# Unread products that shift where each expert's main path begins in TensorE's program

## The chip, the cores and the metric

One of the eight cores of a Trainium2 chip runs the kernel. The time is the device time of one execution, from start to end, in microseconds (us).

## What is computed

One layer of a streaming encoder over 256 tokens of width 1024: a mixer (short convolution, two kinds of attention) and then a mixture of 32 experts, of which each token takes four. The part that matters here is the experts:

```
logits = (xt @ router_w + router_b)
top_vals, top_idx = lax.top_k(logits, 4)
top_w = jax.nn.softmax(top_vals, axis=-1)
combine = jnp.einsum('tk,tke->et', top_w, one_hot(top_idx, 32))
# for each expert e, summed over e:
u = xt @ w1 + b1
a = glu * jax.nn.sigmoid(1.702 * glu) * (lin + 1)     # of the clamped halves of u
acc = acc + gate_e[:, None] * (a @ w2 + b2)
```

Everything is float32. An expert's weights are 12 MB (w1 8 MB, w2 4 MB), and all 32 are read from HBM in every execution.

## The kernel before

The mixer runs first (until about 180 us of the profile), and the weights of the first experts are loaded behind it. Then the 32 experts run one after the other. The router's result is compacted: of each expert the first 64 tokens (CAP) are done by a **main path** that always runs; what is over 64 is done by up to four further blocks (MORE: 32, 64, 64 and 32 slots from slot 64, 96, 160 and 224), each inside the one before it, under a branch on the expert's token count. This whole nest, `if_more`, stands in the program ahead of the expert's main path, so an expert with 64 tokens or fewer jumps over it. Every engine reads the count and branches for itself. TensorE alone gets a hint on the branch (`hint`, a BRANCH_PREFETCH_HINT that says that the jump over the nest is likely to be taken); it stands at the start of the main path of the expert before.

In TensorE's program an expert's section is: the nest (four blocks, never all run), the hint, the bias product (`u<-b,pick`), the first half of w1 (`first`, tiles `u<-we,xg`), for even experts the scatter of the pair before (`y<-o,sc`), the second half of w1, the read of the next expert's count, for odd experts the gather for the next pair (`xg<-oh,xn`), the products with w2 (`o<-we,aT`) with transposes (`aT`) between them, and the next expert's branch. A product of float32 operands stands in the trace as two weight loads and two products, and a transpose or a bias product as one of each.

Weights come in 1 MB transfers from SP's queue (`prefetch`, line 858), 12 for each expert, into a ring of 20 buffers (RING). A transfer is issued when TensorE has read the buffer's last content, and SP's program keeps them in order: while SP waits for one buffer, nothing behind it is issued. The order of instructions is recorded by a scheduler from the Python program; `queue` and `issue_after` pin single steps. The lines are those of the profile: 83 is every product, 86 every transpose, 1021 the branch with its semaphores, 858 the weight transfers.

Of the kernel before, what the change touches and what calls it, by code (L numbers as in the profile page):

```python
# [18 lines left out]
P = 128  # L19
# [13 lines left out]
KINDS = {"l": 7, "h": 8, "x": 2, "c": 3}  # L33
RING = "lhhllccchlhhhxhhlllx"
CAP = 64
MORE = ((64, 32), (96, 64), (160, 64), (224, 32))


# [11 lines left out]
def trunk(ctx: ExitStack, tc: tile.TileContext, x_d, p1_d, p2_d, be_d, ada_d, win_d, wout_d, w1_d, w2_d, out_d):  # L50
# [26 lines left out]
    def pb(name):  # L77
        return psB.tile([P, 512], F32, tag="B", name=name)
# [6 lines left out]
    def turn(out, in_):  # L85
        last[:] = [nc.tensor.transpose(out, in_, ident).ins]  # L86
# [37 lines left out]
    ident = const.tile([P, P], F32, name="ident")  # L124
# [36 lines left out]
    SEL6 = SELE[:, 0:6]  # L161
    slots = const.tile([P, CAP + 32], F32, name="slots")
    iote = const.tile([P, NE], F32, name="iote")
# [565 lines left out]
    def onehot(oh, base, m, es, pos):  # L729

        at = slots[:, base:base + m].rearrange("p (o c) -> p o c", o=1).to_broadcast([P, len(es), m])
        nc.vector.tensor_tensor(oh, at, bcast(pos[:, es[0]:es[0] + len(es)], m), op=ALU.is_equal)

    def gather(ps, oh, t, w, ks=range(KD)):

        for k in ks:
            mm(ps[k * w // 512][:, k * w % 512:k * w % 512 + w], xn2[:, t, k * P:(k + 1) * P], oh.rearrange("p e c -> p (e c)"),
               t == 0 and k * w % 512 == 0, t == NT - 1)

    def modulated2(xg, ps, w):  # L740
        for k in (0, 4, 1, 5, 2, 6, 3, 7):
            o = xg[:, k].rearrange("p e c -> p (e c)")
            x = ps[k * w // 512][:, k * w % 512:k * w % 512 + w]
            if k > 3:
                nc.vector.tensor_scalar(o, x, s2[:, k:k + 1], t2[:, k:k + 1],  # L745
                                        op0=ALU.mult, op1=ALU.add)
            else:
                nc.scalar.activation(o, x, AF.Identity, scale=s2[:, k:k + 1], bias=t2[:, k:k + 1])  # L748
# [10 lines left out]
    class Prepare:  # L759


        def __init__(self, e):
            self.e = e
            self.oh = sm.tile([P, NT, 2, CAP], F32, tag="part", name=f"oh{e}")
            if e:
# [5 lines left out]
        def half(self, t, ks=range(KD)):  # L771
            if 0 in ks:
                onehot(self.oh[:, t], 0, CAP, [self.e, self.e + 1], pos[:, t])
            gather(self.ps, self.oh[:, t], t, 2 * CAP, ks)

        def rest(self):
            e = self.e
            xg = sm.tile([P, KD, 2, CAP], F32, tag="xg", bufs=1, name=f"xg{e}")
            modulated2(xg, self.ps, 2 * CAP)
            og = sm.tile([P, NT, 2, CAP], F32, tag="part", name=f"og{e}")  # L780
# [238 lines left out]

    def if_more(n_e, e, a, aT, blocks=MORE):  # L1020
        with tc.If(n_e > blocks[0][0], label=f"few{e}") if blocks is MORE else tc.If(n_e > blocks[0][0]):  # L1021
            more(e, a, aT, *blocks[0])
            if blocks[1:]:
                if_more(n_e, e, a, aT, blocks[1:])

    @contextmanager
    def behind_branch():
# [19 lines left out]
    def tokens(e):  # L1047

        traced = nc.cur_bb.bb.instructions
        n = len(traced)  # L1050
        value = nc.values_load(cnt[0:1, e:e + 1], min_val=0, max_val=S)
        return value, next(i for i in traced[n:] if i.engine == mybir.EngineType.PE)

    late = None
    n_next, _ = tokens(0)
    for e in range(NE):
        if e:
            prefetch(4)
        xg, sc, _ = ready[e]
        aT = [t1k(f"aT{e}_{G}").rearrange("p (j s) -> p j s", j=2) for G in range(2)]  # L1060
        n_e = n_next
        if_more(n_e, e, t1k(f"am{e}", "partp"), t1k(f"aTm{e}"))
        with behind_branch():
            if e + 1 < NE:
# [27 lines left out]
    o, sc, _ = late  # L1092
# [72 lines left out]
```

## Time and profile before

| what | us |
|---|---|
| median of three runs | 1147.12 |
| lowest and highest run | 1146.0, 1147.28 |
| profiled execution, its own time | 1146.89 |
| its span, first to last instruction | 1144.9 |
| TensorE busy | 1069.5 (93%) |
| mean HBM traffic over the span | 391 GB/s |

The profiled execution's own time is 2.0 us over its span, and 0.23 us under the median. "PEq" in an idle note is TensorE's sequencer: the engine waited for an instruction of line 1021 that the sequencer itself works on. Numbers of experts run from 0 to 31.

### The profile page before, as it was taken

What the parts mean: (1) busy time and instruction counts of PE and PEld (TensorE: products, weight loads), DVE (VectorE), ACT (ScalarE), POOL (GpSimd) and SP (SyncE); (2) the same over time, 40 slices, a digit from 0 to 9 for tenths busy, and PEclk for the clock granted to TensorE, in tenths of its full rate; (3) what the DMA queues carried; (4) which work ended last, traced back from release to release, by engine and by line L of the source; (5) the groups of instructions that cost most, each with busy time, mean ns of one, the idle gap of its engine ahead of it and who ended that gap; (6) DMA issues with size and microseconds to landing.
All of it is one profiled execution on the core that took longest, in us unless ns stands there. A gap on an engine that the chain in (4) does not pass through costs nothing. (4 is left out here: it accounts for less than half of the span.)

```text
span 1144.9 us, 14101 instructions
## 1 busy us (share of the span) xinstructions
PE 1069.5 (93%) x5432; PEld 467.1 (41%) x5432; DVE 389.2 (34%) x879; ACT 178.6 (16%) x412; POOL 14.5 (1%) x52
## 2 busy tenths in 40 slices
PE   2999999999989999999999989999999999898987
PEld 2887844343333333433333433434343434242322
DVE  7799933222232223222222222232232322231222
ACT  3458622010101010101010100101010101010100
POOL 1000000000000000000000000000000000000000
PEclk7899999999999999999999989999999999999999
DMA  9888899999987999999999999999999999999992
GB/s 383 360 297 311 331 409 370 416 418 417 418 353 309 417 418 417 418 418 417 417 418 416 419 399 404 419 418 418 417 417 419 417 418 417 411 416 410 416 413 110
DMA packets 62913, 449.54 MB, mean 393 GB/s; under 512 B 6960, under 2 KB 7472, under 8 KB 8624
## 3 DMA queue, kind: packets, MB, share of 16 engines
q1 hardware_dynamic: 62336, 447.11, 95.6%
q8 instruction: 79, 1.29, 0.5%
q10 hardware_dynamic: 432, 0.59, 0.1%
q14 instruction: 66, 0.54, 0.1%
HBM read 446.63 MB, written 1.05 MB: 391 GB/s over the span
## 5 line engine op out<-in xcount | busy, mean ns | idle before, releaser
L83 PE MATMUL u<-we,xg 128*64 128x512 f32 (+1 forms) x2304 | 494.2, 577 | 12.7 <-DMA we<-in_w 11.3
L83 PEld LDWEIGHTS u<-we,xg 128*64 128x64 f32 (+1 forms) x2304 | 154.0, 134 | 299.9 <-issue 260.4
L83 PE MATMUL o<-we,aT 128*64 128x512 f32 x1024 | 236.5, 598 | 3.7 <-DMA we<-in_w 3.3
L891 DVE TENSOR_SCALAR sw<-u 128x256 f32<-128x256 f32 (+1 forms) x68 | 28.3, 417 | 441.6 <-PE u L83 429.5
L892 ACT ACTIVATE sw<-sw 128x256 f32<-128x256 f32 (+1 forms) x68 | 27.9, 411 | 666.8 <-DVE sw L891 666.8
L83 PEld LDWEIGHTS o<-we,aT 128*64 128x64 f32 x1024 | 69.6, 136 | 133.2 <-issue 121.8
L1088 DVE TENSOR_TENSOR o<-o,g 64x512 f32<-64x512 f32 x64 | 44.1, 689 | 162.2 <-PE o L83 161.7
L83 PE MATMUL y<-o,sc 128*128 128x512 f32 (+1 forms) x160 | 67.1, 592 | 2.1 <-DVE o L1010 1.3
L83 PEld LDWEIGHTS xg<-oh,xn 128*128 128x128 f32 x512 | 58.6, 192 | 12.6 <-issue 12.4
L83 PE MATMUL xg<-oh,xn 128*128 128x128 f32 x512 | 62.1, 279 | 0.1
L236 DVE SCALAR_TENSOR_TENSOR a<-a,silurow 128x1024 f32<-128x1024 f32 x48 | 57.2, 1216 | 0.0
L745 DVE TENSOR_SCALAR xg<-xg,mods 128x128 f32<-128x128 f32 x64 | 26.0, 410 | 62.7 <-ACT xg L748 61.5
L83 PE MATMUL u<-b,pick 128*128 128x512 f32 x64 | 31.0, 484 | 17.3 <-PEq L1021 16.7
L83 PEld LDWEIGHTS y<-o,sc 128*128 128x128 f32 (+1 forms) x160 | 26.5, 197 | 41.8 <-issue 33.4
L944 DVE TENSOR_TENSOR xr<-xr,y 128x1024 f32<-128x1024 f32 x30 | 36.6, 1221 | 11.8 <-PE y L83 10.4
L904 ACT COPY aT<-aT 128x256 f32<-128x256 f32 x64 | 23.8, 372 | 106.1 <-PE aT L86 106.0
L748 ACT ACTIVATE xg<-xg,mods 128x128 f32<-128x128 f32 x64 | 28.9, 457 | 56.4 <-PE xg L83 45.9
L83 PEld LDWEIGHTS u<-b,pick 128*128 128x128 f32 x64 | 12.1, 189 | 57.1 <-issue 55.9
L86 PEld LDWEIGHTS aT<-ident,a 128*128 128x128 f32 x128 | 14.2, 141 | 50.7 <-issue 33.9
L895 DVE TENSOR_TENSOR a<-a,sw 128x256 f32<-128x256 f32 x64 | 27.4, 428 | 6.8 <-ACT sw L892 0.3
L86 PE MATMUL aT<-ident,a 128*128 128x128 f32 x128 | 27.2, 294 | 2.0
L83 PE MATMUL op<-o,yT 128*128 128x512 f32 x64 | 29.0, 600 | 0.0
(299 smaller groups left out, 750.3 us busy)
## 6 DMA issues: line engine op xcount, KB each, us to landing
we<-in_w SPq DMA_DIRECT2D x383, 1024.0 KB, 19.9
a<-in_ada SPq DMA_DIRECT2D x24, 1024.0 KB, 7.0
w<-in_win SPq DMA_DIRECT2D x12, 1024.0 KB, 11.0
o<-in_wout SPq DMA_DIRECT2D x4, 1024.0 KB, 5.8
xr<-in_x SPq DMA_DIRECT2D x1, 1024.0 KB, 5.3
we<-in_w SPq DMA_DIRECT2D x2, 512.0 KB, 18.1
b1in<-in_be SPq DMA_DIRECT2D x1, 512.0 KB, 5.3
out<-xr SPq DMA_DIRECT2D x2, 256.0 KB, 2.0
```

What stands on the lines that cost most here:

```text
L83: last[:] = [nc.tensor.matmul(out, lhsT, rhs, start=start, stop=stop, skip_group_check=True).ins]
L86: last[:] = [nc.tensor.transpose(out, in_, ident).ins]
L236: nc.vector.scalar_tensor_tensor(w[:, i], w[:, i], 1.0, silu_row, op0=ALU.mult, op1=ALU.mult, accum_out=mods[:, m, k:k + 1])
L745: nc.vector.tensor_scalar(o, x, s2[:, k:k + 1], t2[:, k:k + 1], op0=ALU.mult, op1=ALU.add)
L748: nc.scalar.activation(o, x, AF.Identity, scale=s2[:, k:k + 1], bias=t2[:, k:k + 1])
L891: nc.vector.tensor_scalar(gl, u[:, 0:n], 7.0, None, op0=ALU.min)
L892: nc.scalar.activation(sg, gl, AF.Sigmoid, scale=1.702)
L895: nc.vector.tensor_mul(ln, ln, sg)
L904: nc.scalar.copy(aT.rearrange("p j s -> p (j s)"), ps[:, 0:n])
L944: nc.vector.tensor_add(xr[:, t, :], xr[:, t, :], y.rearrange("p h m -> p (h m)"))
L1088: nc.vector.tensor_mul(o[64 * (e % 2):64 * (e % 2) + 64, 512 * h:512 * h + 512], ps[r, :], g2[r, :])
```

## The change

At the end of the innermost block of an expert's nest (the one that runs only with more than 224 of the 256 tokens) the changed kernel writes a number of transposes of the identity into a PSUM tile, `fill`, that nothing reads. The number comes from a table by expert:

```
+FILL = (99, 1, 77, 100, 92, 116, 91, 116, 91, 116, 91, 116, 91, 116, 91, 116, 91, 116, 91, 116, 91, 116, 91, 116, 91, 116, 91, 116, 91, 116, 91, 0)
...
             if blocks[1:]:
                 if_more(n_e, e, a, aT, blocks[1:])
+            elif FILL[e]:
+                fill = pb(f"fill{e}")
+                for _ in range(FILL[e]):
+                    turn(fill[:, 0:P], ident)
```

Sum of the table: 3,060 transposes. The rows of DVE, ScalarE, GpSimd and SP are the same in both programs but for line numbers. Counted in the built programs with the trace's ratio (a float32 product is four instructions, a transpose or a bias product two), the main paths of neighbouring experts from expert 4 on stand 1,808 and 1,858 instructions apart by turns before, and 2,040 apart now; a main path is 230 instructions for an even expert and 280 for an odd one. An instruction that the built program does not list is in none of these counts.

First place: TensorE's program at the end of expert 5's nest and the start of its main path. Names end in the program's buffer numbers: `o_224` and `y_224` are the innermost block's products, `u_0` the main path's first. Before:

```order
L83 MATMUL o_224_5767<-we_10_5296,aTm_5330 32x256 x8
L83 MATMUL o_224_5767<-we_11_5298,aTm_5330 32x256 x8
L83 MATMUL y_224_00_5895<-o_224_5890,sc_224_5743 128x256 x2
L83 MATMUL y_224_01_5899<-o_224_5890,sc_224_5743 128x256 x2
L83 MATMUL y_224_10_5903<-o_224_5890,sc_224_5743 128x256 x2
L83 MATMUL y_224_11_5907<-o_224_5890,sc_224_5743 128x256 x2
L1021 UNCONDITIONAL_BRANCH x5
L1161 BRANCH_PREFETCH_HINT
L83 MATMUL u_0_5912<-b_222,pick_4568 128x512
```

The same place now:

```order
L89 MATMUL fill_6285<-ident 128x128 x4
L86 MATMUL o_224_6141<-we_10_5670,aTm_5704 32x256 x8
L86 MATMUL o_224_6141<-we_11_5672,aTm_5704 32x256 x8
L89 MATMUL fill_6285<-ident 128x128 x5
L86 MATMUL y_224_00_6269<-o_224_6264,sc_224_6117 128x256 x2
L89 MATMUL fill_6285<-ident 128x128 x3
L86 MATMUL y_224_01_6273<-o_224_6264,sc_224_6117 128x256 x2
L86 MATMUL y_224_10_6277<-o_224_6264,sc_224_6117 128x256 x2
L86 MATMUL y_224_11_6281<-o_224_6264,sc_224_6117 128x256 x2
L89 MATMUL fill_6285<-ident 128x128 x104
L1024 UNCONDITIONAL_BRANCH x5
L1168 BRANCH_PREFETCH_HINT
```

The 116 transposes stand between and behind the innermost block's products, all ahead of its closing branch; the hint and the main path behind it follow unchanged, 232 instructions further on.

Second place: the same end of the nest for expert 10, on TensorE. Before:

```order
L83 MATMUL y_224_10_9550<-o_224_9537,sc_224_9390 128x256 x2
L83 MATMUL y_224_11_9554<-o_224_9537,sc_224_9390 128x256 x2
L1021 UNCONDITIONAL_BRANCH x5
L1161 BRANCH_PREFETCH_HINT
L83 MATMUL u_0_9559<-b_222,pick_8924 128x512
```

Now:

```order
L86 MATMUL y_224_10_10459<-o_224_10446,sc_224_10299 128x256 x2
L86 MATMUL y_224_11_10463<-o_224_10446,sc_224_10299 128x256 x2
L89 MATMUL fill_10467<-ident 128x128 x79
L1024 UNCONDITIONAL_BRANCH x5
L1168 BRANCH_PREFETCH_HINT
```

Here 79 of the 91 transposes stand behind the last product (12 stand further up), and again nothing of the main path is moved against anything else of it.

## Rows read from the trace of the kernel before

**Rows 1.** The page's second part: the span in 40 equal slices of 28.6 us, TensorE's busy tenths and what the DMA engines moved.

```profile
PE   2999999999989999999999989999999999898987
...
GB/s 383 360 297 311 331 409 370 416 418 417 418 353 309 417 418 417 418 418 417 417 418 416 419 399 404 419 418 418 417 417 419 417 418 417 411 416 410 416 413 110
```

**Rows 2.** Busy time by stretch: from and to in us, length, then busy us and instructions of each engine, TensorE's granted clock, the DMA engines' busy share and GB/s.

```profile
183.00:323.00 140.00, 138.35 (x621) 52.27 (x620) 34.24 (x80) 14.38 (x34) 2.54 (x6) 1.00 1.00 411
323.00:345.00 22.00, 17.78 (x247) 8.89 (x245) 9.74 (x23) 1.42 (x5) 0.00 (x0) 1.00 0.74 306
345.00:349.00 4.00, 4.00 (x13) 1.21 (x14) 1.19 (x6) 0.00 (x0) 0.00 (x0) 0.57 0.01 2
349.00:481.00 132.00, 130.10 (x607) 50.59 (x605) 33.87 (x76) 13.96 (x35) 1.59 (x6) 1.00 1.00 411
481.00:514.00 33.00, 29.81 (x129) 10.07 (x127) 8.77 (x17) 1.58 (x4) 0.00 (x0) 1.00 1.01 417
...
640.00:709.00 69.00, 59.84 (x418) 24.18 (x418) 20.11 (x47) 5.39 (x15) 0.00 (x0) 0.93 1.00 405
709.00:980.00 271.00, 266.71 (x1221) 100.01 (x1217) 70.00 (x153) 25.88 (x65) 2.67 (x10) 1.00 1.01 418
```

**Rows 3.** What SP's queue waited for from 324 to 349 us: total us, times, longest us.

```profile
SPq L858 <- PE u L83: 24.2, 1, 24.2
```

**Rows 4.** The branch's line over the whole span, TensorE's sequencer (duration ns, least, median, most) and who waited for the line; and from the groups of instructions the only products with the nest's tile `aTm`.

```profile
L1021 PEldq COMPARE_BRANCH  x36: 74/348/6017, 181.2 to 1104.2; - x36
...
  PE u L83: 16.7, 30
...
L83 PE MATMUL o<-we,aTm 128*32 128x256 f32 x128 | 8.2, 383 | 4.2 <-DMA we<-in_w 3.1 <-ACT aTm L904 0.7 <-ACTq L1021 0.4
```

**Rows 5.** Who waited for the branch's line: in the waits from 183 to 349 us (two rows), then in those from 349 to 980 us. Total us, times, longest us.

```profile
PE u L83 <- PEq L1021: 1.8, 4, 0.7
...
PE o L83 <- PEq L1021: 0.3, 1, 0.3
...
PE u L83 <- PEq L1021: 12.6, 21, 2.0
```

**Rows 6.** TensorE in order of time, the first instructions behind the branches of experts 1 to 5 and what follows expert 5's: start us, us, engine, line, tiles, shapes, count, in brackets the idle time before and what ended it.

```profile
206.78 3.64 PE L83 MATMUL o<-we,aT 128*64 128x512 f32 x14 [0.28 <-PEq L1021]
...
238.60 0.47 PE L83 MATMUL u<-b,pick 128*128 128x512 f32 x1 [0.40 <-PEq L1021]
...
268.64 0.49 PE L83 MATMUL u<-b,pick 128*128 128x512 f32 x1 [0.30 <-PEq L1021]
...
296.90 0.47 PE L83 MATMUL u<-b,pick 128*128 128x512 f32 x1 [0.41 <-PEq L1021]
...
323.00 1.07 PE L83 MATMUL xg<-xn,ox 128*32 128x256 f32 x16
...
344.68 0.47 PE L83 MATMUL u<-b,pick 128*128 128x512 f32 x1 [0.67 <-PEq L1021]
345.08 8.75 PE L83 MATMUL u<-we,xg 128*64 128x512 f32 x32
```

**Rows 7.** TensorE in order of time behind the branches of experts 10, 11 and 17, and the branch instruction of TensorE's sequencer in the stretches 395 to 402 us, 478 to 487 us and 506 to 514 us (duration ns three times, start us).

```profile
485.82 0.47 PE L83 MATMUL u<-b,pick 128*128 128x512 f32 x1 [1.99 <-PEq L1021]
...
513.05 0.47 PE L83 MATMUL u<-b,pick 128*128 128x512 f32 x1 [1.06 <-PEq L1021]
...
708.18 0.47 PE L83 MATMUL u<-b,pick 128*128 128x512 f32 x1 [2.03 <-PEq L1021]
...
L1021 PEldq COMPARE_BRANCH  x1: 348/348/348, 396.3 to 396.3; - x1
...
L1021 PEldq COMPARE_BRANCH  x1: 6017/6017/6017, 479.4 to 479.4; - x1
...
L1021 PEldq COMPARE_BRANCH  x1: 5092/5092/5092, 507.5 to 507.5; - x1
```

**Rows 8.** TensorE in order of time at the starts of the main paths of experts 6 and 8.

```profile
374.57 0.47 PE L83 MATMUL u<-b,pick 128*128 128x512 f32 x1 [0.41 <-PEq L1021]
...
429.38 0.47 PE L83 MATMUL u<-b,pick 128*128 128x512 f32 x1 [0.41 <-PEq L1021]
```

**Rows 9.** TensorE in order of time in the nest of expert 16.

```profile
652.23 1.06 PE L83 MATMUL xg<-xn,ox 128*32 128x256 f32 x12 [1.20 <-issue]
...
665.32 1.07 PE L83 MATMUL o<-we,aTm 128*32 128x256 f32 x16 [0.52 <-DMA we<-in_w]
...
667.91 1.07 PE L83 MATMUL o<-we,aTm 128*32 128x256 f32 x16 [1.26 <-DMA we<-in_w]
670.31 1.07 PE L83 MATMUL o<-we,aTm 128*32 128x256 f32 x16 [1.33 <-DMA we<-in_w]
```

**Rows 10.** The chain that ended last, in order of time: start us, us, what.

```profile
1112.57 19.88 DMA we<-in_w
...
1132.58 3.67 PE o L83 x16
```

**Rows 11.** The page's third part, the queue of 16 KB instruction packets (packets, MB, share of 16 DMA engines), and the last 22 us of weight traffic by stretch, columns as in rows 2.

```profile
q8 instruction: 79, 1.29, 0.5%
...
1110.00:1121.50 11.50, 9.31 (x39) 3.04 (x36) 1.61 (x4) 0.79 (x2) 0.00 (x0) 1.00 0.93 370
1121.50:1132.00 10.50, 9.13 (x39) 2.37 (x35) 1.60 (x4) 0.79 (x2) 0.00 (x0) 1.00 0.07 28
```

## The prediction

> **What bounds the kernel now.** I read the 40 slices first [rows 1]. TensorE stands at nine tenths almost everywhere, which alone would make it the suspect, but the GB/s row says otherwise: from the eighth slice on it lies at 416 to 418, with two dips, slices 12 and 13 (353 and 309) and 24 and 25 (399 and 404). So the experts' stage is two machines running side by side, and what matters is which one waits for the other at each place.
>
> The stretches make that sharp [rows 2]. From 345 to 349 us the DMA engines move 2 GB/s and TensorE is busy all the time. SP's queue waited once, 24.2 us, for TensorE to read a w1 buffer [rows 3]: expert 5 has over 64 tokens, TensorE went through the first block of its nest from 323.00 to about 344, main path 5 began at 344.68 [rows 6], and only its first products freed the next buffer. Up to there **TensorE sets the pace**: a microsecond won or lost ahead of 344.68 moves the restart of the weights, and all behind it, by a microsecond. After it the weights run at 411 to 418 GB/s and TensorE's delays do not reach them [rows 2], and the chain that ended last is one weight transfer after another, followed by the last products [rows 10]. From 349 us on **the weights set the pace**.
>
> The spare time of TensorE there: two main paths take 429.38 - 374.57 = 54.8 us [rows 8], their 24 transfers of 1.049 MB take 25.17 MB / 417 GB/s = 60.4 us [rows 2]. So TensorE gains 5.6 us a pair until it has caught up.
>
> **The change, part by part.** *The transposes.* They stand in a block for more than 224 tokens. The branch's line ran 36 times in TensorE's sequencer, 32 first tests and four more, and the only products with the nest's tile are 128 of the 32-wide block, 64 for each of two experts [rows 4]. So two experts entered the first block and none the second; the 3,060 transposes cost 0 us of execution. Other engines' programs are the same, and no queue is passed.
>
> *The positions.* What is left is where a main path starts in TensorE's program, so what its sequencer pays at the branch. Line 1021 made products wait 16.7 us, 30 times [rows 4]; that is all there is to win, and nearly all of it lies where it buys nothing:
> - Ahead of 344.68 there are five such places: 0.28, 0.40, 0.30, 0.41 and 0.67 us [rows 6], 2.06 together. The first four agree with the waits' two rows, 1.8 with the last of them and 0.3 apart [rows 5].
> - From 349 to 980 there are 21, 12.6 us together [rows 5]. Three are long, 1.99, 1.06 and 2.03 [rows 7]; the other 18 average (12.6 - 5.08) / 18 = 0.42.
>
> Is 0.4 us the price of a position? I think not. Where the branch took the sequencer 0.348 us, at 396.3, main path 7 began some five microseconds later with an ordinary gap; where it took 6.017 and 5.092 us the gaps were 1.99 and 1.06 [rows 7]. A quick branch lies well ahead of the products, so 0.4 us is what remains when its target is at hand: the sequencer still waits until the products ahead have ended. The long branches are the ones that a better position could cure: 1.59, 0.66 and 1.63 us over the floor of 0.4, 3.9 us in all. But they stand at 485.82, 513.05 and 708.18. At the first two the weights moved at 417 GB/s throughout [rows 2] and TensorE catches up 5.6 us a pair anyway. The third lies in the 640 to 709 stretch, at 405 GB/s, but behind the dip that expert 16's nest makes, and is likewise ahead of 271 us at 418. I book 0 for them.
>
> *Expert 16's nest.* One 1.20 us gap there is ended by nothing that the profile shows, where its program runs on into the nest although the hint said jump [rows 9]. A moved start may remove it or make it longer. Behind it in the same nest TensorE waited 0.52 + 1.26 + 1.33 = 3.11 us for weights [rows 9], so a gain of 1.20 is taken back there, and a loss hits TensorE while weights are late: 0 us, with 1 us at most either way.
>
> *Bounds for the five early branches.* Below: the whole 2.06 us gone, or more soberly 0.27, the last one's excess over 0.4. Above: each pays what the worst branch pays, 2.03: 5 x 2.03 - 2.06 = 8.1 us. The nearest rows are the 18 ordinary ones, from experts whose starts differ by 1,808 or 1,858 instructions and so stand at many positions; and the five themselves show no long one. I take 0.
>
> Sum: the profiled execution's 1146.89 + 0 = 1146.9; the median is 0.23 us higher, so **1147.1** as a median.
>
> **The rivals.** [...]
>
> [...]
>
> *B, fewer fetches help the last DMA engine (faster).* In the last 10.5 us of weights the traffic is 28 GB/s [rows 11]; 418 / 16 is 26, so one engine of sixteen is still at work when the others are done. Instruction packets take DMA time as well: 0.5% of 16 engines over 1144.9 us is 92 us, 1.16 us for each of 79 [rows 11]. If paths that begin on an edge need, say, 16 packets fewer and these all came off that engine, it would end up to 10.5 us earlier: 1136.6. If they are spread over sixteen it is 16 x 1.16 / 16 = 1.2 us, 1145.9. No row says on which engine they run, and that all hit the one that is late needs luck.
>
> [...]
>
> **How the numbers follow.** No change, rival C within 0.2% included: 0.76, of which C holds about a third. Rival A from 3.3 us: 0.15, and C or an unlucky clock (granted 0.57 behind expert 5's nest [rows 2]) over 2.3 us: 0.02. Rival B over 2.3 us: 0.07. A measurement of this kernel can tell about 0.2%, 2.3 us, from no change. That makes faster 0.07, same 0.76, slower 0.17. The range begins at the bound of the five branches, 1147.1 - 2.06 = 1145.0, and ends where the first step of A stands, 1150.4; beyond it lie the rest of A and of B, about 0.18.
>
> **What would show it.** Right: the restart of the weights stays within 0.5 us of 349, the products behind 344.68's counterpart have a gap of 0.4 to 0.7, line 1021's total may fall from 16.7 to about 13 with no gap over 1 us, and the weights' last landing stays at 1132. [...] Wrong by B: the restart unmoved, the last stretch at 28 GB/s shorter than 10.5 us, and the end earlier by that much.

## Result and profile after

The changed kernel takes 1154.26 us (median of 8 runs, 1149.56 to 1155.52) against 1147.2 of the kernel before on the same chip: ratio 1.0053, 95% interval 1.0036 to 1.007. It is **slower by half a per cent**, outside the predicted range. The profiled execution took 1153.15 us with a span of 1151.1, 6.2 us more than before. Lines have moved: 86 is every product, 89 every transpose, 861 the weight transfers and 1024 the branch.

The first places to read are the five early branches and the start of main path 5, TensorE in order of time, columns as in [rows 6]:

```profile
203.15 2.79 PE L86 MATMUL o<-we,aT 128*64 128x512 f32 x10
210.06 5.34 PE L86 MATMUL o<-we,aT 128*64 128x512 f32 x14 [4.12 <-PEq L1024]
...
243.59 0.47 PE L86 MATMUL u<-b,pick 128*128 128x512 f32 x1 [0.41 <-PEq L1024]
...
273.63 0.50 PE L86 MATMUL u<-b,pick 128*128 128x512 f32 x1 [0.30 <-PEq L1024]
...
301.89 0.47 PE L86 MATMUL u<-b,pick 128*128 128x512 f32 x1 [0.41 <-PEq L1024]
...
350.19 0.76 PE L86 MATMUL u<-b,pick 128*128 128x512 f32 x1 [0.66 <-PEq L1024]
```

Four of the five gaps are what they were. The first, behind main path 0, was 0.28 us and is 4.12, and the 14 products behind it take 5.34 us in place of 3.64 [rows 6]. That is 3.84 + 1.70 = 5.54 us, and main path 5 starts 350.19 - 344.68 = 5.51 us later. That the two agree so closely is partly luck: this execution was 0.56 us ahead of the other when its last ten products ahead of the gap began (203.15 against 203.71), so it is 4.99 us late at 243.59, 273.63 and 301.89, and loses 0.52 us more on its way to main path 5, which I did not assign.

The branch itself, on TensorE's sequencer, took 0.430 us before:

```profile
L1024 PEldq COMPARE_BRANCH  x1: 6016/6016/6016, 203.7 to 203.7; - x1
```

The stretches of the kernel after, columns as in [rows 2], say why the products are slower and where the loss goes:

```profile
205.00:210.00 5.00, 0.94 (x4) 0.06 (x1) 0.10 (x1) 0.00 (x0) 0.00 (x0) 1.00 1.01 410
210.00:215.00 5.00, 4.94 (x14) 1.50 (x14) 1.09 (x6) 0.00 (x0) 0.00 (x0) 0.66 0.59 208
215.00:329.00 114.00, 112.63 (x525) 43.81 (x524) 29.74 (x64) 10.41 (x26) 1.06 (x4) 1.00 1.00 409
329.00:350.00 21.00, 17.07 (x232) 8.69 (x228) 8.59 (x22) 1.42 (x5) 0.00 (x0) 0.94 0.67 277
350.00:356.00 6.00, 5.81 (x19) 1.86 (x21) 1.45 (x7) 0.00 (x0) 0.00 (x0) 0.65 0.10 12
356.00:488.00 132.00, 130.11 (x607) 49.94 (x605) 33.85 (x76) 13.95 (x35) 1.59 (x6) 1.00 1.01 415
```

The granted clock is 0.66 right behind the gap, from 210 to 215 us, where it was 1.00 before. Weights dip to 208 GB/s there, where they were at 423; TensorE frees no buffer while it stands, and from 200 to 222 us SP's queue waits up to 7.5 us at a time for products of `o`, where it was 3.9 at most. The stretch with almost no traffic is now 350 to 356 instead of 345 to 349 [rows 2], and from there the weights run at 415 to 418 GB/s again, but for 640 to 715 us (383), with the loss on top.

The branch's line over the whole span, answering [rows 4], then the waits for it from 354 to 980 us, answering [rows 5]:

```profile
L1024 PEldq COMPARE_BRANCH  x36: 74/356/6088, 180.7 to 1110.4; - x36
...
  PE u L86: 18.6, 30
...
  PE o L86: 4.8, 3
```

```profile
PE u L86 <- PEq L1024: 14.4, 21, 6.2
```

Of the 4.8 us ahead of `o`, TensorE's own sequencer has 4.12, the gap behind main path 0; the rest is ScalarE's branch. Together that is 18.6 + 4.12 = 22.7 us. Two gaps make the difference, 4.12 and the 6.24 us that main path 16 waits behind its nest; without them it is 12.4. The three long gaps of [rows 7] are cured, each main path now starting with an ordinary one:

```profile
489.95 0.47 PE L86 MATMUL u<-b,pick 128*128 128x512 f32 x1 [0.41 <-PEq L1024]
516.53 0.47 PE L86 MATMUL u<-b,pick 128*128 128x512 f32 x1 [0.41 <-PEq L1024]
...
687.83 0.77 PE L86 MATMUL u<-b,pick 128*128 128x512 f32 x1 [6.24 <-PEq L1024]
...
716.45 0.47 PE L86 MATMUL u<-b,pick 128*128 128x512 f32 x1 [0.40 <-PEq L1024]
```

### The profile page after: what moved, and what is told of

Read it like the earlier page. It is cut to its first block, busy times and chain, and to the rows that moved or that the text cites. A ratio compares the mean times of both kernels' runs of the same rounds, so it can differ in the third digit from the quotient of the medians.

```text
span 1151.1 us, 14100 instructions
## 1 busy us (share of the span) xinstructions
PE 1070.7 (93%) x5432; PEld 466.5 (41%) x5432; DVE 389.1 (34%) x879; ACT 178.6 (16%) x412; POOL 14.4 (1%) x52
## 3 DMA queue, kind: packets, MB, share of 16 engines
q8 instruction: 76, 1.25, 0.4%
## 5 line engine op out<-in xcount | busy, mean ns | idle before, releaser
L86 PEld LDWEIGHTS xg<-oh,xn 128*128 128x128 f32 x512 | 58.6, 192 | 12.6 <-issue 12.4
L86 PE MATMUL u<-b,pick 128*128 128x512 f32 x64 | 31.3, 490 | 19.2 <-PEq L1024 18.6
```

What stands on the lines that cost most here:

```text
L86: last[:] = [nc.tensor.matmul(out, lhsT, rhs, start=start, stop=stop, skip_group_check=True).ins]
```

## Experiments

The profiled executions, with the ratio to the kernel before where it was timed. "Branch 1" is the branch that closes main path 0, "gap 1" the wait behind it, "start 5" the start of main path 5, which stands for the restart of the weights. In the expectations an "edge" is a place at which the change puts the start of a main path, and places are counted in instructions from it, two for a transpose. Their theories suppose that the program is fetched in blocks, one of which begins at an edge. The traces show packets of about 16 KB on the instruction queue q8 (76 in the kernel after, 1.25 MB); where a block begins and how many instructions it holds no run shows.

| kernel | branch 1, us | gap 1, us | start 5 | time, us (runs) | ratio, 95% |
|---|---|---|---|---|---|
| before | 0.430 | 0.28 | 344.68 | 1147.2 (8) | 1 |
| after | 6.016 | 4.12 | 350.19 | 1154.26 (8) | 1.0036 to 1.007 |
| undo_first | 0.339 | 0.28 | 345.14 | 1148.37 (11) | 0.9997 to 1.0022 |
| first_alone | 6.316 | 4.42 | 351.14 | 1154.05 (8) | 1.0041 to 1.0082 |
| target_moved | 6.112 | 4.21 | 351.98 | 1154.97 (4) | 1.0045 to 1.0075 |
| path0_8later | 6.492 | 4.67 | 350.71 | 1153.88 (1) | |
| path0_16later | 6.232 | 4.41 | 351.13 | 1154.37 (1) | |
| path0_later | 0.430 | 0.28 | 344.84 | 1146.9 (10) | 0.9984 to 1.0002 |
| path0_48later | 0.430 | 0.28 | 345.94 | 1148.52 (1) | |
| no_hint1 | 6.182 | 4.28 | 352.48 | 1154.69 (5) | 1.0034 to 1.0072 |

**Undo one entry (undo_first).**

```diff
-FILL[0:3] = 99, 1, 77
+FILL[0:3] = 0, 100, 77
```

> The table's first entry goes back from 99 to 0 and the second from 1 to 100: main path 0 starts where it did before the change, main path 1 and all behind it stay within one instruction of where the change has put them. Theory L (main path 0, 206 instructions long, lies inside one block when it starts at an edge, so the target of the branch that closes it is not there in time): the 4.12 us gap ahead of the first w2 products near 210 is 0.3 to 0.4, the clock behind it stays at 1.00, the weights restart at 349 +- 0.7 in place of 354.5, and the time is 1147.0 to 1148.7. Rival T (it is main path 1's own place, the target on an edge, that makes this branch long): the gap stays at 4, the time at 1153 to 1154.5. Rival N (the branch near 210 is only a symptom and the time is lost in expert 16's nest, where TensorE waits 6.24 us): gap gone, restart at 349, time still 1152 to 1154.

Gap 0.28, main path 5 back at 345.14, the time that of before. That is what Theory L forecast, and T and N fall: main path 1 stands where the change puts it, and so does main path 15, a place at which main path 16 waits 6.24 us in the kernel after and 6.08 in path0_later, which also has the time of before.

**One entry alone (first_alone).**

```diff
-FILL = (99, 1, 77, 100, ...)
+FILL = (99, 0, 0, 0, ...)
```

> Only the first entry, 99, is left of the table; the other 31 are 0, so main path 0 starts where the change puts it and all later paths slide as they did before the change. Theory L: the gap behind main path 0 is 4.1, clock about 0.6 behind it, restart 354.5, time 1152.6 to 1154.3. Rival T: main path 1 still stands where the change puts it within two instructions, so the same; it does not tell L from T. Rival N: gap 4, but the time 1147 to 1148.5, since expert 16's nest lies elsewhere.

One number of the 32 makes the whole loss: ratio 1.0061 beside the full change's 1.0053.

**The target moved 128 instructions on (target_moved).**

```diff
-FILL[0:3] = 99, 1, 77
+FILL[0:3] = 99, 65, 13
```

> [...] Theory L: nothing changes for the branch behind main path 0: gap 4.1, restart 354.5, time 1153 to 1155. Rival T: the gap falls to 0.3 to 0.5, restart 349, time 1147 to 1148.7.

Main path 1 stands 64 transposes, 128 instructions, further on, main path 0 and main path 2 where the change puts them. The branch still takes 6.112 us. Moving the target by that much does not matter; T falls a second time.

**Main path 0 further on (four kernels).**

```diff
-FILL[0:2] = 99, 1
+FILL[0:2] = 103, 125    # path0_8later
+FILL[0:2] = 107, 121    # path0_16later
+FILL[0:2] = 111, 117    # path0_later
+FILL[0:2] = 123, 105    # path0_48later
```

Main path 0 counts 206 instructions. Here it starts 8, 16, 24 and 48 instructions behind the edge and ends 214, 222, 230 and 254 behind it; main path 1 and all behind it move on by 128 transposes in all four.

> [...] With 24 behind the edge the long branch was gone. Theory L narrow (the fetch starts when the reading of the program comes within some distance of the block's end, and 206 is just too short): this tells where the point lies; gap 4.1 (time 1153 to 1155) if it lies above 214, 0.3 (1147 to 1148.5) if below. Rival (only a start exactly on the edge is bad): 0.3.

> First entry 107, second 121: main path 0 starts 16 instructions behind the edge and ends 222 behind it. With 8 behind (end 214) the branch behind it was long, with 24 (end 230) it was not. Theory L narrow: the point lies between 214 and 230, so either is possible here: gap 4 to 4.7 and 1153 to 1155, or 0.3 and 1146.5 to 1148.5; a gap in between (1 to 3) would say that the fetch starts here, but late.

> [...] Theory L in its narrow form (the end of the path decides, 206 is too early and 230 late enough): gap 0.3 to 0.5, restart 349 +- 0.7, time 1147.0 to 1148.7. Theory L in its wide form (any place at which the path stays inside one block): gap 4, restart 354.5, time 1153 to 1155. Rival T: as the wide form.

> [...] Theory L narrow (only the distance of the path's end from the block's end decides): gap 0.3, restart 349 +- 0.7, time 1146.5 to 1148.5. Theory L wide (a path that stays inside its block misses its target): gap 4, 1153 to 1155.

With its end 206, 214 and 222 instructions behind the edge the branch is long, 6.016, 6.492 and 6.232 us, with 230 and 254 it is short, 0.430 both times, and there is nothing in between. So for main path 0 it is not one exact starting place; it fits that what counts is how far on the path ends, as the narrow form has it. The wide form's gap of 4 us did not come, 0.28 both times; that it is wrong rests on those two ends lying inside a block, which is not shown. Nor is it shown that the end decides and not the start: the path's start, with the hint, moves along with its end. A longer path at an edge is main path 6 of the kernel after, 230 instructions, so that it ends 24 further on than main path 0, and the branch that closes it is short:

```profile
L1024 PEldq COMPARE_BRANCH  x1: 352/352/352, 402.1 to 402.1; - x1
```

The instruction packets of queue q8 go with this. The queues from 195 to 204 us, then 204 to 210, of the kernel after, and from 195 to 204.4 us, all ahead of the branch, of path0_later:

```profile
q1 hardware_dynamic: 519, 3.83, 101.7%
...
q8 instruction: 1, 0.02, 1.1%
```

```profile
q1 hardware_dynamic: 533, 3.93, 99.9%
q8 instruction: 1, 0.02, 0.7%
```

In the kernel after no packet comes in the 9 us ahead of the branch, and one comes while the branch runs, between 207 and 207.5 us; in path0_later it comes ahead, and the branch takes 0.43 us. In the kernel before one comes between 200 and 200.5 us, ahead of its short branch at 204.3. In path0_16later none comes from 186 to 203.5 us and one from 203.5 to 211, and its branch takes 6.232 us.

**No hint for that branch, in the kernel before (no_hint1).**

```diff
-if e + 1 < NE:
+if 0 < e < NE - 1:
     hint(e + 1)
```

> The kernel before, without the change, but without the hint that stands at the start of main path 0 (the one for the branch that closes it). If the change's long branch behind main path 0 is a target that has not been fetched, a branch that no hint announces must cost the same: branch 6.0 us, gap 4.1 to 4.5 ahead of the w2 products near 210, clock about 0.6 to 0.8 just behind, restart of the weights 354 to 355, time 1152.5 to 1154.5. Rival: the hint does nothing for this branch, and what the change does to it is something else: gap 0.28 as before, time 1147 to 1148.

The branch line's answer from 200 to 212 us, and TensorE behind it:

```profile
L1021 PEldq COMPARE_BRANCH  x1: 6182/6182/6182, 204.9 to 204.9; - x1
```

```profile
211.37 6.21 PE L83 MATMUL o<-we,aT 128*64 128x512 f32 x14 [4.28 <-PEq L1021]
```

Without its hint the unchanged kernel does what the changed one does: branch and gap agree to 0.2 us, and the products behind are slow, 6.21 us in place of the 5.34 of the changed kernel. The change left the hint in the program, but the branch costs what it costs without one.

**No hint for the branch ahead of main path 3 (no_hint3).**

```diff
-if e + 1 < NE:
+if e + 1 < NE and e != 2:
     hint(e + 1)
```

> The kernel before without the hint at the start of main path 2, for the branch ahead of main path 3 (268.64 before). Theory Q (a long branch costs its 6 us less the products that TensorE still has queued when the branch begins: 24 w2 products, 5.4 us, behind an ordinary path, but only 10, 2.8 us, behind main path 0): gap 1.7 to 2.2 there in place of 0.30, no fall of the clock, restart 350.2 to 351, time 1148.4 to 1149.6. Rival P (every long branch ahead of the restart costs what main path 0's did, 5.5 us): gap 4 and a fall of the clock, time 1152.5 to 1154.5.

TensorE in order of time:

```profile
270.18 0.49 PE L83 MATMUL u<-b,pick 128*128 128x512 f32 x1 [1.83 <-PEq L1021]
...
275.64 7.92 PE L83 MATMUL u<-we,xg 128*64 128x512 f32 x27 [3.54 <-issue]
...
306.12 0.47 PE L83 MATMUL u<-b,pick 128*128 128x512 f32 x1 [2.22 <-PEq L1021]
...
355.59 0.76 PE L83 MATMUL u<-b,pick 128*128 128x512 f32 x1 [0.66 <-PEq L1021]
```

Ratio 1.0101 (1.008 to 1.0123), 1158.98 us: both expected times were too low. The gap itself is Theory Q's, 1.83 us for a branch of 5.97. Why main path 0's is larger can be read in the kernel before: the last products ahead of the branch of main path 0, and of main path 6, an ordinary one:

```profile
203.71 2.79 PE L83 MATMUL o<-we,aT 128*64 128x512 f32 x10
...
395.37 5.37 PE L83 MATMUL o<-we,aT 128*64 128x512 f32 x24
```

Ten products, 2.79 us, cover the branch behind main path 0, since 14 of its w2 products stand behind the branch; 24, or 5.37 us, cover an ordinary one. The other two idle times I did not foresee: 2 us into main path 3 TensorE stood for 3.54 us, ended by nothing that the profile shows (one packet of q8 comes between 270 and 276 us; whether TensorE waited for it is not shown), and the branch ahead of main path 4, 3.181 us in the kernel before, took 6.248. Excess gaps of 1.53 + 3.54 + 1.81 = 6.88 us leave some 4 of the 10.91 us by which main path 5 is late; the clock, 0.94 on average from 270 to 323 where it was 1.00, goes with them, but I did not separate it.

**No hints in the late stretch (no_hints_late).**

```diff
-if e + 1 < NE:
+if e + 1 < NE and not 6 <= e < 15:
     hint(e + 1)
```

> The kernel before without the hints for the branches ahead of main paths 7 to 15, all in the stretch where the weights set the pace. Theory W (a late TensorE costs nothing there while it loses less than the 5.6 us that a pair of paths has to spare): nine gaps of about 2 us in place of 0.4, about 14 us more idle time on TensorE between 395 and 630, restart unmoved at 349, time 1146.5 to 1148.7. Rival (idle time of TensorE counts wherever it is): 1159 to 1163.

Ratio 1.0092 (1.0068 to 1.0115), 1159.32 us. Stretches of this kernel, then of the kernel before:

```profile
389.00:640.00 251.00, 230.01 (x1020) 85.28 (x1018) 59.54 (x132) 21.53 (x54) 2.14 (x8) 0.97 1.01 412
640.00:700.00 60.00, 52.93 (x405) 22.34 (x401) 17.19 (x43) 5.03 (x14) 0.53 (x2) 0.96 0.80 328
```

```profile
389.00:640.00 251.00, 244.44 (x1116) 91.29 (x1113) 64.76 (x147) 22.71 (x57) 2.66 (x10) 1.00 1.01 418
640.00:700.00 60.00, 53.00 (x389) 21.95 (x387) 17.30 (x39) 5.01 (x14) 0.00 (x0) 0.91 0.99 403
```

Theory W's zero is refuted for nine gaps: the gaps were 1.7 to 2.55 us, but with the clock and further waits the four pairs from main path 7 to main path 15 took 645.86 - 402.19 = 243.7 us, 60.9 a pair, just over the 60.4 of the transfers; before it was (622.65 - 401.15) / 4 = 55.4. So 5.5 of the 5.6 us that a pair has to spare were gone, and TensorE began main path 15 23.2 us later, with nothing in hand for expert 16's nest; there the weights, which need its buffers, fell to 328 GB/s in place of 403. An estimate from these rows: 6 GB/s less over 251 us are 3.6 us at 417 GB/s, 75 less over 60 us are 10.8, together 14.4 of the 14.9 us by which this execution's span is longer. By it most of the loss lies in the nest, not in the pairs.

**Expert 16's nest (main15_moved).**

```diff
-FILL[0:2], FILL[15:17] = (99, 1), (116, 91)
+FILL[0:2], FILL[15:17] = (111, 117), (132, 75)
```

> The table with 111 and 117 at its start, as in the run that cured the branch behind main path 0, and main path 15 moved 32 instructions behind the edge (132 in place of 116, then 75 in place of 91), with all others in place. In every kernel with main path 15 on an edge the unannounced jump at the end of the first block of expert 16's nest took 6.0 us and main path 16 waited 5.5 to 6.2 us; in the kernel before, with main path 15 elsewhere, it took 0.33. Theory F (the hint's target, main path 16, has then been fetched early in main path 15 and is still there after the nest): jump 0.33, gap ahead of main path 16 0.66, 5.4 us less idle time on TensorE. Theory W (behind the restart that is worth nothing, since one weight engine's backlog ends last): time 1146.0 to 1148.0, as without this step. Rival: the 5.4 us count, and the time is 1141 to 1143.

The branch's line and the start of main path 16, from 672 to 690 us:

```profile
L1024 PEldq COMPARE_BRANCH  x2: 207/314/420, 677.0 to 677.9; - x2
```

```profile
678.39 0.76 PE L86 MATMUL u<-b,pick 128*128 128x512 f32 x1 [0.72 <-PEq L1024]
```

The long jump is gone, 0.42 us in place of 6.007 in path0_later, and the gap 0.72 in place of 6.08. The time is not better: 1148.1 us, ratio 1.0007 (0.9999 to 1.0016), beside 0.9993 for path0_later. Stretches of main15_moved, then of path0_later:

```profile
640.00:700.00 60.00, 51.34 (x379) 21.42 (x379) 15.85 (x34) 4.61 (x13) 0.00 (x0) 0.91 0.99 403
...
1120.00:1130.00 10.00, 8.79 (x36) 2.88 (x34) 1.69 (x5) 0.79 (x2) 0.00 (x0) 1.00 0.31 116
1130.00:1136.00 6.00, 5.25 (x26) 1.70 (x24) 0.64 (x2) 0.37 (x1) 0.00 (x0) 1.00 0.07 28
```

```profile
640.00:700.00 60.00, 45.42 (x350) 17.81 (x351) 15.43 (x33) 4.61 (x13) 0.00 (x0) 0.89 0.94 378
...
1120.00:1130.00 10.00, 8.80 (x36) 2.94 (x36) 1.66 (x5) 0.79 (x2) 0.00 (x0) 1.00 0.44 177
1130.00:1136.00 6.00, 5.25 (x25) 1.61 (x22) 0.00 (x0) 0.37 (x1) 0.00 (x0) 1.00 0.06 25
```

The weights move faster in the nest, 403 against 378 GB/s, and slower in 1120 to 1130; in the last stretch both have about one sixteenth of the traffic left, 28 and 25 GB/s where 418 / 16 is 26. The 5.4 us are worth nothing at the end: W holds for a single gap. That one transfer engine's backlog is the reason is argued from the last stretch, not tested.

This pair of kernels shows one thing more. The two tables differ in entries 15 and 16 alone, and their sum is the same, so main paths 16 to 31 stand where they stood. Yet the branch that closes main path 17 takes, in path0_later and then in main15_moved:

```profile
L1024 PEldq COMPARE_BRANCH  x1: 3066/3066/3066, 734.5 to 734.5; - x1
```

```profile
L1024 PEldq COMPARE_BRANCH  x1: 340/340/340, 731.8 to 731.8; - x1
```

In the kernel after, whose table differs from that of path0_later in its first two entries alone, the branches that close the odd paths from 17 to 29 take 2.91 to 3.70 us. The place in the program does not settle a branch by itself; what ran before counts too. Ahead of main path 0 the kernels compared are alike but for its place.

No version beats both kernels. The best, path0_later, takes the change's loss away, and its interval against the kernel before holds 1.

## Why the prediction was wrong

**The bound was right.** Until the weights' restart TensorE sets the pace: 5.51 us lost ahead of main path 5 are 6.25 us at the end of the span. In the table every kernel with a long branch 1 has main path 5 at 350 to 352.5 and 1153.9 to 1155.0 us, every one without at 344.7 to 346 and 1146.9 to 1148.5. The last 0.7 us I can't assign; the runs differ by more. One reading was loose: from the eighth slice on, outside the two dips and the last slice, the GB/s row lies at 410 to 419, not 416 to 418; nothing hangs on it.

**The step that failed** is the one on the five early branches: bounds of minus 2.06 and plus 8.1, "I take 0". Two reasons carried it, and both were unsound. The 18 ordinary gaps came from other paths at many positions, but main path 0 stands at one, and is 24 instructions shorter than the even paths that I reasoned with. And "the five themselves show no long one" was evidence for the starts before, which the change's first entry moves; besides, it was read off the gaps, and one of the five branches was long in the kernel before, the one ahead of main path 4:

```profile
L1021 PEldq COMPARE_BRANCH  x1: 3181/3181/3181, 292.1 to 292.1; - x1
```

Its gap is an ordinary 0.41 [rows 6], so a gap of 0.4 us does not show that a branch's target was at hand, as the prediction took it. In place of the 0 the runs showed a branch of 6.016 us behind main path 0, a gap of 4.12 in place of 0.28, and 1.70 us of slower products behind it. The count that would have pointed to main path 0, 206, was to be had from the program.

**Rival A had part of the outcome, not the place or the price.** A long branch ahead of the restart did come, for which I gave A a chance of 0.15. But only the one behind main path 0 cost a gap; those behind main paths 1 and 2 took 0.337 and 0.336 us, and so short, 0.430, is the one behind main path 0 when the path ends at 230 or 254. Behind the odd paths the branches did become long, 2.87 to 3.70 us behind each from 3 to 29 but 15 (whose branch isn't taken), and the products queued ahead cover them. A's price, 1.63 us, came from a branch with 24 products queued ahead of it; here 10 were queued, so the gap is 4.12, and the clock takes another 1.70. The range's end, 1150.4, which is 1147.1 and two such prices, and the third of the 0.76 that C holds both use the paths' places in blocks, a term that no run shows; in its place the runs showed one long branch, which cost 5.5 us with the clock behind it. A branch without a hint took 6.18 us in no_hint1 and 5.97 in no_hint3, and the change, with its 6.016, shows that a hint alone does not make it short.

**Zeros that held.** The transposes never run. The three long gaps of [rows 7] were cured, and the kernels with that cure and a short branch 1 are no faster than before. Expert 16's nest I bounded by 1 us; the 1.20 us at its start are gone without effect, while the gap behind the jump out of it, which I had not priced, grew by 5.6 us (0.66 to 6.24) and was free as well, as main15_moved shows. no_hints_late shows where such zeros end: there the pairs used up their spare time, and expert 16's nest was no longer free.

**Rivals B and C.** There are 76 instruction packets where 79 were [rows 11], not 16 fewer, and no early end, so B falls. C, by which long branches would merely fall on other experts, falls because no gap of 1 to 2 us appears at other experts and the durations repeat from pair to pair: 2.87 to 3.70 us for the branch that closes an odd path from 3 on, 0.33 to 0.36 for one that closes an even path from 6 on.

**Open.** What in a path's place makes its branch long: the five places only put the change between an end at 222 and one at 230, and for main path 0 alone. The long branches of other paths that does not explain: one of 6.017 us closes main path 9 in the kernel before [rows 7], 280 instructions long, and the odd paths of the changed kernel, as long, have branches of 2.87 to 3.70 us, of which that of main path 17 is short in main15_moved, 0.340, without the path being moved. What the late packet holds is open as well: in no_hint1 one comes between 186 and 203.5 us, ahead of the branch at 204.9, and that branch is long all the same, and a packet's content is not in the trace.

## What to carry to other kernels

When code is shifted, look at the one path that differs from the rest (here the first, shorter by 24 instructions), and only then at the regular ones. A long branch costs its own time less the work queued ahead of it, plus what the clock takes afterwards: here 6.016 us left a gap of 4.12 behind ten products, 1.70 us of slower products came on top, and behind 24 products a branch of 5.97 us left 1.83. Here a single one counted only ahead of the point at which the weights take over; behind that point nine of them counted again, when the spare time was used up. A prefetch hint in the program is no proof of a short branch (6.016 us with it, 6.182 without), and neither is an ordinary gap (0.41 us behind a branch of 3.181): read the branch's duration.

## What the runs showed of the hardware

- The branch behind main path 0 takes 0.34 to 0.43 us in four kernels of the table and 6.02 to 6.49 in six; the change from long to short lies between path ends 8 instructions apart (222 and 230). The branches without a hint take 6.18 us in no_hint1, 5.97 in no_hint3 and up to 6.68 in no_hints_late. Elsewhere in the kernels before and after there are durations in between, 1.87 to 5.09 us, so it is not a matter of two values.
- Some long branches cost no gap: in the kernel after, those that close main paths 3 and 5 take 2.87 us (at 297.0) and 3.56 us (at 375.5), and the products queued ahead cover them: 0.41 us is left at 301.89; the page's gaps alone would not show them.
- The same branch at the same place in the program can be long or short: 3.07 us behind main path 17 in path0_later, 0.34 in main15_moved.
- An idle time of 4.12 us in the kernel after was followed by a granted clock of 0.66 from 210 to 215 us, one of 4.41 in path0_16later by 0.50, and the 14 products behind such an idle time took 5.34 us in the kernel after and 6.21 in no_hint1, in place of 3.64; behind the nine gaps of 1.7 to 2.55 us in no_hints_late the mean was 0.97 where it had been 1.00.
- After a jump without a hint TensorE can stand a second time: in no_hint3 2 us into the path and for 3.54 us, longer than the 1.83 at the jump, and in no_hints_late 4 us into main path 8 for 1.35 us. Nothing that the profile shows ends these.
